# Token sums of the FFN: the eight additions of hi and lo on GpSimd instead of VectorE

## The chip, the cores and the metric

The kernel runs on one core of one Trainium2 chip. The metric is the device time of one execution in microseconds (us), the median over runs. A core has a matrix engine (TensorE, PE in the profile; PEld is its loading of weights), a vector engine (VectorE, DVE), an activation engine (ScalarE, ACT), a general engine (GpSimd, POOL) and an engine that here only issues DMAs (SyncE, SP). Each works through its own queue in order; between the queues semaphores hold an instruction until what it needs is there.

## What is computed

A trunk of two layers over 512 tokens of width 1024: a token mixer (dilated attention in layer 0, a gated recurrence in layer 1) and behind each a gated FFN with a causal convolution of three taps. The change lies in the two FFNs alone:

```python
def conv_ffn(x, w_up, conv_w, conv_b, w_down):
    u = causal_dwconv(x @ w_up, conv_w, conv_b)
    g, v = u[..., :D_FF], u[..., D_FF:]
    return (jax.nn.gelu(g, approximate=True) * v) @ w_down
```

with `D_FF` = 3072, so `x @ w_up` is 512 x 1024 by 1024 x 6144.

## The kernel before

**Numbers in two parts.** Each float32 operand is split into hi, a rounded copy that TensorE multiplies at full speed, and lo, what is left: `split` (lines 148 to 150) copies hi on ACT (L149) and subtracts on DVE (L150). A product is three matmuls, hi by hi, hi by lo and lo by hi (`mm3`, `PASSES`). The normalized tokens lie turned, features on partitions, in the pair `hT`; weights come from DRAM as `raw` and are split into `whi` and `wlo`.

**Products with seven multiplications.** Of the 24 chunks of `w_up`, the first 6 are multiplied plainly (`feat_tiles`, `tiles`; L412). The other 18, the "chains", are cut into two by two blocks and multiplied in seven steps instead of eight (Strassen's scheme in Winograd's form): `chain` (lines 1010 to 1045), run by `seven` (lines 1047 to 1094), matmuls at L1023. The right factors of four of the seven steps are not blocks of the tokens but sums and differences of blocks. They are the same for all chains and are made once in each FFN by `token_sums` (lines 918 to 978). With the four blocks of the tokens, B11 (features 0 to 511, tokens 0 to 255), B12, B21 and B22, each of two tiles of 128x512, it goes through these steps:

- L939, in `both`: each of the eight tiles of the B's is put together as hi + lo from `hT` (`whole` makes the two tiles of a block);
- L957: b11 = B11 - B12, split into the pair T0, right factor of step 5 (`parted(0)`);
- L964 and L945: b12 = B22 - B12 and b22 = -b11 - B22 in turn; b22 is split into T1, factor of step 6 (`parted(1)`), and b12 into T2, factor of step 7 (`parted(2)`);
- L976, run as L945 by the helper `negative`: b21 = -b22 - B21, split into T3, factor of step 4 (`parted(3)`).

The tiles that hold T0 to T3 (`homes`) take the place of the residual stream `x_sb`, which is copied to DRAM first by a DMA from POOL's queue (`x_kept`, L923).

**What sets the order.** The order on every engine is that in which the program issues (`tc.manual_schedule()`). `token_sums` is a side routine: `side` puts it into a list with a delay, and every `tick` (lines 377 to 386), called once for each tile of output, counts the delays down and lets a side routine that is due issue its next part, up to its next `yield n`, which says after how many ticks it goes on. Behind the side routines `tick` calls `pump`, which splits the next weights into free slots and starts loads. In an FFN `token_sums` starts at the fifth tick (line 830). The first eight ticks are two passes over four tiles, one for each half of the tokens (`feat_tiles` with `halves`); six ticks of one full tile each follow (`tiles`, line 831 on), and then `seven` starts. In `seven` the steps of a chain stand at the slots `AT = {1: 0, 5: 1, 2: 2, 6: 4, 3: 5, 7: 8, 4: 13}`.

**The work around it.** A finished tile of `x @ w_up` goes through `begin`: ACT evacuates the bank and applies the third tap (L773, tile `u`), DVE adds the other two taps from the bank (L777, two instructions), then either ACT applies the gelu (L795), or DVE multiplies by the gate (L799). In a chain, L1032 copies the result of step 1 (`part`) out of the bank before step 6 adds onto it; `across` (L210) and `lower` (L214) sum blocks of the raw weights on DVE, and `add_rows` (L186) adds rows to raw weights by an accumulating DMA issued from POOL.

Of the kernel before, what the change touches and what calls it, by code (L numbers as in the profile page):

```python
# [11 lines left out]
F32 = mybir.dt.float32  # L12
# [3 lines left out]
ALU = mybir.AluOpType  # L16
# [67 lines left out]
def kernel(  # L84
# [25 lines left out]
    nc = tc.nc  # L110
# [12 lines left out]
    def nm(s):  # L123
        uid[0] += 1
        return f"{s}{uid[0]}"

    def gen(dt=F32, s="g"):
        return gp.tile([P, 512], dt, tag="g", name=nm(s))
# [19 lines left out]
    def split(hi, lo, raw):  # L148
        nc.scalar.activation(hi, raw, AF.Copy)  # L149
        nc.vector.tensor_tensor(lo, raw, hi.bitcast(F32), op=ALU.subtract)  # L150
# [613 lines left out]
    def ffn(layer, hT, post, pre):  # L764
# [63 lines left out]
        up["direct"] = direct  # L828
        T = []
        side(token_sums(hT, T), 5)  # L830
        for j in range(SEVEN[0] - 1):
            if j:
# [85 lines left out]
    def token_sums(hT, T, first=False):  # L918

        if not first:  # L920
            assert len(sides) == 1, len(sides)
            d = dp.tile([P, 4, D], F32, name=nm("x_kept"))
            nc.gpsimd.dma_start(d, X[0])  # L923
            kept.append(d)
        homes = cp.tile([P, 4, D], F32R, tag="x_sb", name=nm("T"))
        homes = [homes[:, n] for n in range(4)]
        homes += [cp.tile([P, D], F32R, tag="gain", name=nm("T"), bufs=2) for _ in range(1 if first else 2)]
        homes = [[h[:, 0:512], h[:, 512:1024]] for h in homes]
        if first:
            homes += [[gen(F32R, "T") for _ in range(2)]]  # L930
        homes += [[wp.tile([P, 512], F32R, tag=t, name=nm("T")) for _ in range(2)] for t in ("hi", "lo")]
        state["live"] += 2
        homes = [[h.rearrange("p (k t) -> p k t", k=2) for h in hs] for hs in homes]
        yield 1 + first

        def both(k0, n):
            o = gen(s="B").rearrange("p (k t) -> p k t", k=2)
            hi, lo = (h[:, k0 : k0 + 2, n * 256 : n * 256 + 256] for h in hT)
            tt(o, hi.bitcast(F32), lo.bitcast(F32), op=ALU.add)  # L939
            return o  # L940

        tt = nc.vector.tensor_tensor

        def negative(o, a, b):
            nc.vector.scalar_tensor_tensor(o, a, -1.0, b, op0=ALU.mult, op1=ALU.subtract)  # L945

        def whole(k0, n):
            return [both(k0 + 2 * k, n) for k in range(2)]

        def parted(n, b):  # L950
            for k in range(2):
                split(homes[2 * n][k], homes[2 * n + 1][k], b[k])

        b11, b12 = whole(0, 0), whole(0, 1)
        yield 1 + first
        for k in range(2):
            tt(b11[k], b11[k], b12[k], op=ALU.subtract)  # L957
        parted(0, b11)
        yield 1 + first
        b22 = whole(4, 1)  # L960
        if not first:
            yield 1
        for k in range(2):
            tt(b12[k], b22[k], b12[k], op=ALU.subtract)  # L964
            negative(b22[k], b11[k], b22[k])
        yield 1 + first
        parted(1, b22)
        T.extend([homes[2 * n], homes[2 * n + 1]] for n in range(4))
        yield 1 + first
        parted(2, b12)  # L970
        yield 1 + first
        b21 = whole(4, 0)
        if first:
            yield 2
        for k in range(2):
            negative(b21[k], b22[k], b21[k])  # L976
        yield 1 + first
        parted(3, b21)
# [117 lines left out]
    def attention(hT, post, pre):  # L1096
# [359 lines left out]
        for hp in range(4):  # L1456
            q, k = [], []
            if hp % 2 == 0:
                v = []
                values(v) if hp else first_values(v)  # L1460
            if hp == 0:
                side(build)
                side(token_sums(hT, T, True), 2)
            sink = qk_sink(q, k)
            if hp < 3:
                feat_tiles(2, hT, sink)
                for hh in range(2):
                    side(local(2 * hp + hh, hh, q, k, v), 1 + hh)
# [252 lines left out]
```

## Time and profile before

| | |
|---|---|
| median of 3 runs | 1420.02 us (1419.88 to 1420.48) |
| the profiled execution | 1420.89 us |
| its span, first to last instruction | 1419.1 us |
| mean granted TensorE clock | 0.998 |
| additions at L939, DVE | 24 (8 in attention, 8 in each FFN), 684 ns each in the middle |
| token sums' instructions, first FFN | 512.6 to 547 us of the span |
| the same, second FFN | 1054.3 to 1089 us |

A line of the profile's timeline has the start in us from the first instruction, the time that a merged group of instructions spans, the engine, the line of the kernel, the operation, the written tile `<-` the tiles read, their shapes and how many instructions are merged; in brackets stands how long the engine was idle before, and which engine's instruction ended that. A line of the view of waits has the waiting engine and line, what it waited for, and then the total in us, the number of waits and the longest one. A line of the groups has after the bar the busy time in us, the mean in ns, and the idle time ahead.

### The profile page before, as it was taken

The page shows a single profiled execution, that of the slowest core. Times are in us where ns is not written, and L with a number is a line of the kernel's source. Part 1 is how long each engine was busy: PE and PEld are TensorE (multiplying, and loading weights), DVE is VectorE, ACT ScalarE, POOL GpSimd, SP SyncE. Part 2 cuts the span into 40 slices and gives each one's busy share as a digit, 9 for nine tenths or more (in the row PEclk, how much of TensorE's full clock was granted, in tenths as well). Part 3 has the DMA queues.
Part 4 walks back from the last instruction along what each step waited for, and adds up shares of the span by engine and source line. Part 5 has one row for each costly group of instructions (what it writes and reads, how often), then busy time and mean ns, then how long its engine had stood idle before and what let it go on. Part 6 is the DMA issues. An engine that isn't in the chain of part 4 may idle for free.

```text
span 1419.1 us, 23634 instructions
## 1 busy us (share of the span) xinstructions
PE 1406.0 (99%) x8741; PEld 1267.6 (89%) x8741; DVE 1125.1 (79%) x2201; ACT 800.6 (56%) x1646; POOL 225.8 (16%) x344
## 2 busy tenths in 40 slices
PE   9999999999999999999999999999999999999998
PEld 7888999999998898999999888888898999999886
DVE  6676898887866988998888758769789898888843
ACT  7343565353636555666666645589455666666641
POOL 0441332131300102221110001000101212111000
PEclk9999999999999999999999999999999999999999
DMA  7643464655655445666663632431435757665411
GB/s 227 181 145 110 122 178 150 174 162 162 177 184 186 160 149 115 152 153 159 128 151 89 212 129 90 134 119 63 145 127 113 171 118 164 153 130 127 165 58 60
DMA packets 171886, 201.93 MB, mean 142 GB/s; under 512 B 10561, under 2 KB 141081, under 8 KB 171513
## 3 DMA queue, kind: packets, MB, share of 16 engines
q1 hardware_dynamic: 123064, 153.34, 33.8%
q0 software_dynamic: 47856, 46.02, 17.6%
q8 instruction: 69, 1.13, 0.3%
q10 hardware_dynamic: 848, 1.05, 0.2%
q14 instruction: 49, 0.39, 0.1%
HBM read 181.41 MB, written 18.96 MB: 141 GB/s over the span
## 4 chain that ended last, share of the span: by engine, by line
PE 83%; DVE 9%; ACT 5%; issue 1%; DMA 0%; POOL 0%; DVEq 0%; ACTq 0%
PE ps L1023 35%; PE acc L412 25%; PE ps L412 11%; PE v L1219 7%; DVE wlo L150 3%; DVE u L777 2%; PE v L1157 1%; DVE xb L1524 1%; PE O L1431 1%; PE S L1365 1%; ACT whi L149 1%; PE S L1313 1%; DVE T L150 1%; DVE B L939 1%; ACT sig L1545 1%
## 5 line engine op out<-in xcount | busy, mean ns | idle before, releaser
L150 DVE TENSOR_TENSOR wlo<-raw,whi 128x512 fp32r<-128x512 f32 x620 | 410.7, 686 | 112.1 <-ACT whi L149 109.5
L149 ACT ACTIVATE whi<-raw 128x512 fp32r<-128x512 f32 x620 | 371.0, 626 | 189.3 <-PE ps L1023 76.3
L1023 PE MATMUL ps<-T,whi 128*128 128x256 f32 x1664 | 304.3, 283 | 4.2 <-ACT part L1032 3.5
L412 PE MATMUL ps<-hT,whi 128*128 128x512 f32 (+1 forms) x1088 | 288.0, 353 | 0.0
L1023 PEld LDWEIGHTS ps<-T,whi 128*128 128x128 f32 x1664 | 259.3, 190 | 8.9 <-ACT part L1032 3.9
L1023 PE MATMUL ps<-T,wlo 128*128 128x256 f32 x832 | 233.3, 280 | 0.0
L1023 PE MATMUL ps<-hT,whi 128*128 128x256 f32 x1248 | 231.4, 284 | 0.0
L412 PEld LDWEIGHTS ps<-hT,whi 128*128 128x128 f32 x1088 | 190.8, 189 | 26.4
L1023 PEld LDWEIGHTS ps<-hT,whi 128*128 128x128 f32 x1248 | 196.6, 192 | 2.6
L412 PE MATMUL ps<-hT,wlo 128*128 128x512 f32 (+1 forms) x544 | 191.3, 352 | 0.0
L1023 PE MATMUL ps<-hT,wlo 128*128 128x256 f32 x624 | 176.8, 283 | 0.0
L186 POOL DMA_DIRECT2D raw<-in_ffn_w_up_dram x72 | 92.8, 1318 | 424.4 <-DVE wlo L150 291.2
L1023 PEld LDWEIGHTS ps<-T,wlo 128*128 128x128 f32 x832 | 158.4, 190 | 0.0
L412 PE MATMUL acc<-whi,ahi 128*128 128x512 f32 x352 | 137.7, 391 | 0.0
L412 PE MATMUL acc<-whi,alo 128*128 128x512 f32 x352 | 137.2, 390 | 0.2
L412 PE MATMUL acc<-wlo,ahi 128*128 128x512 f32 x352 | 137.0, 389 | 0.0
L1023 PEld LDWEIGHTS ps<-hT,wlo 128*128 128x128 f32 x624 | 119.8, 192 | 0.0
L412 PEld LDWEIGHTS ps<-hT,wlo 128*128 128x128 f32 x544 | 102.9, 189 | 14.0
L1219 PE MATMUL v<-whi,hT 128*128 128x512 f32 x320 | 106.5, 396 | 0.0
L1032 ACT ACTIVATE part<-ps 128x256 f32<-128x256 f32 x156 | 58.7, 376 | 71.7 <-PE ps L1023 68.7
L777 DVE SCALAR_TENSOR_TENSOR u<-ps,cols,u 128x511 f32<-128x511 f32 x120 | 89.4, 746 | 5.0 <-ACT u L773 2.9
L412 PEld LDWEIGHTS acc<-whi,alo 128*128 128x128 f32 x352 | 66.1, 188 | 14.9 <-DVE alo L150 1.1
(206 smaller groups left out, 2125.5 us busy)
## 6 DMA issues: line engine op xcount, KB each, us to landing
raw<-in_ffn_w_up_dram SPq DMA_DIRECT2D x48, 1024.0 KB
raw<-in_attn_w_qkv_dram SPq DMA_DIRECT2D x67, 512.0 KB
raw<-in_ffn_w_up_dram POOLq DMA_DIRECT2D x72, 256.0 KB, 4.9
raw<-in_ffn_w_down_dram SPq DMA_DIRECT2D x14, 1024.0 KB
dw<-in_ffn_w_down_dram SPq DMA_DIRECT2D x40, 256.0 KB
raw<-in_lru_w_in_dram SPq DMA_DIRECT2D x8, 1024.0 KB
turned<-T POOLq DMA_DIRECT2D x26, 256.0 KB, 2.6
ft<-turned POOLq DMA_DIRECT2D x104, 64.0 KB, 4.6
```

What stands on the lines that cost most here:

```text
L149: nc.scalar.activation(hi, raw, AF.Copy)
L150: nc.vector.tensor_tensor(lo, raw, hi.bitcast(F32), op=ALU.subtract)
L186: nc.gpsimd.dma_start(to, src, accum_op=ALU.add)
L412: mm(dst, l[a], r[b], start=start and n == 0, stop=stop and n == 2)
L777: nc.vector.scalar_tensor_tensor(u[:, d:], ps[:, : S - d], wc, u[:, d:], op0=ALU.mult, op1=ALU.add)
L939: tt(o, hi.bitcast(F32), lo.bitcast(F32), op=ALU.add)
L1023: mm(dst, W[wa][0][:, k, :], right[n](ha, k), start=n in (1, 5) and k == q == 0, stop=k == 3 and q == 2, skip_group_check=True,)
L1032: later(1, lambda: nc.scalar.activation(to, dst, AF.Copy))
L1157: mm(banks[t], hT[a][:, k, t * P : (t + 1) * P], W[b][k % 2][:, 0, :], start=u == n == 0, stop=u == 3 and n == 5,)
L1219: mm(bank, hT[a][:, k, t * P : (t + 1) * P], W[b][k % 2][:, 0, :], start=(k, a, b) == (0, 0, 0), stop=(k, a, b) == (KD - 1, 1, 0),)
L1313: mm(Sp[a // 2][:, o + lo : o + 256], q[hh][:, a * P : (a + 1) * P], k[hh][:, k0 : (a + 1) * P], start=True, stop=True)
L1365: mm(ps[:, c], q[hh][:, c], k[hh][:, c], start=True, stop=True)
```

## The change

In the calls from the two FFNs (`first` is False) the eight additions are issued on `nc.gpsimd` instead of `nc.vector`, all eight at the tick at which `token_sums` starts, directly behind the `x_kept` DMA on POOL's queue. The order is B11, B12, B22, B21. The other steps follow from two ticks later on, one step to a tick: b11 - b12 at the tick of before, and from b22 - b12 on each a tick earlier than before. In the call from attention (`first` is True) the engine, the order and the ticks are as they were.

```diff
         homes = [[h.rearrange("p (k t) -> p k t", k=2) for h in hs] for hs in homes]
-        yield 1 + first
+        if first:
+            yield 2
 
         def both(k0, n):
             o = gen(s="B").rearrange("p (k t) -> p k t", k=2)
             hi, lo = (h[:, k0 : k0 + 2, n * 256 : n * 256 + 256] for h in hT)
-            tt(o, hi.bitcast(F32), lo.bitcast(F32), op=ALU.add)
+            (nc.vector if first else nc.gpsimd).tensor_tensor(o, hi.bitcast(F32), lo.bitcast(F32), op=ALU.add)
             return o
...
         b11, b12 = whole(0, 0), whole(0, 1)
-        yield 1 + first
+        if not first:
+            b22, b21 = whole(4, 1), whole(4, 0)
+        yield 2
         for k in range(2):
             tt(b11[k], b11[k], b12[k], op=ALU.subtract)
         parted(0, b11)
         yield 1 + first
-        b22 = whole(4, 1)
-        if not first:
-            yield 1
+        if first:
+            b22 = whole(4, 1)
         for k in range(2):
             tt(b12[k], b22[k], b12[k], op=ALU.subtract)
             negative(b22[k], b11[k], b22[k])
...
         parted(2, b12)
         yield 1 + first
-        b21 = whole(4, 0)
         if first:
+            b21 = whole(4, 0)
             yield 2
         for k in range(2):
             negative(b21[k], b22[k], b21[k])
```

## The prediction

> **What bounds the kernel now.** I read the page first, then TensorE's waits over the whole run.
>
> ```profile
> span 1419.1 us, 23634 instructions
> PE 1406.0 (99%) x8741; PEld 1267.6 (89%) x8741; DVE 1125.1 (79%) x2201; ACT 800.6 (56%) x1646; POOL 225.8 (16%) x344
> ```
>
> ```profile
> PE ps L1023 <- ACT part L1032: 3.5, 2, 1.8
> PE warm L1640 <- DVE one L1685: 1.5, 1, 1.5
> PE ps L1023 <- DVE ps L1041: 0.7, 1, 0.7
> PE v L1157 <- DVE wlo L150: 0.2, 1, 0.2
> ```
>
> TensorE is busy 99% of the span and is named in four rows of waits only. Work taken off VectorE (DVE) is therefore worth something only where it shortens one of them. The first row is two stalls of 1.8 us, one in each FFN, and both stand right behind the token sums that the change touches. TensorE's timeline shows them:
>
> ```profile
> 550.07 0.40 PE L1023 MATMUL ps<-hT,whi 128*128 128x256 f32 x2
> ...
> 552.36 0.50 PE L1023 MATMUL ps<-T,whi 128*128 128x256 f32 x2 [1.77 <-ACT part L1032]
> ...
> 553.77 0.63 PE L1023 MATMUL ps<-T,whi 128*128 128x256 f32 x2
> ...
> 554.41 0.63 PE L1023 MATMUL ps<-hT,whi 128*128 128x256 f32 x2
> ...
> 556.83 0.40 PE L1023 MATMUL ps<-T,whi 128*128 128x256 f32 x2
> ```
>
> ```profile
> 1091.39 0.40 PE L1023 MATMUL ps<-hT,whi 128*128 128x256 f32 x2
> ...
> 1091.75 0.40 PE L1023 MATMUL ps<-hT,whi 128*128 128x256 f32 x2
> ...
> 1094.03 0.50 PE L1023 MATMUL ps<-T,whi 128*128 128x256 f32 x2 [1.77 <-ACT part L1032]
> ...
> 1096.98 0.40 PE L1023 MATMUL ps<-T,whi 128*128 128x256 f32 x2
> ```
>
> A group of three matmuls (two with whi, one with wlo) starts each 0.36 us (1091.39, 1091.75). So the group of 552.36 was due at 550.43 and is 1.93 late; that of 1094.03 was due at 1092.11 and is 1.92 late. In the first FFN the next eight groups take 4.47 us (552.36 to 556.83), in the second 2.95 (1094.03 to 1096.98): behind the first stall a group takes 0.64 us (553.77, 554.41), the clock having dropped, and that costs another 1.52. **All that the change can win is 1.93 + 1.52 + 1.92 = 5.4 us.**
>
> What ends the stall is read on ScalarE (ACT) and DVE:
>
> ```profile
> 546.43 0.64 ACT L795 ACTIVATE u<-u 128x512 f32<-128x512 f32 x1 [1.48 <-DVE u L777]
> 546.97 0.76 ACT L773 ACTIVATE u<-ps,cols 128x512 f32<-128x512 f32 x1
> ...
> 549.38 0.64 ACT L149 ACTIVATE whi<-raw 128x512 fp32r<-128x512 f32 x1 [1.13 <-DVE raw L214]
> 550.88 0.63 ACT L795 ACTIVATE u<-u 128x512 f32<-128x512 f32 x1 [0.87 <-DVE u L777]
> ...
> 551.94 0.36 ACT L1032 ACTIVATE part<-ps 128x256 f32<-128x256 f32 x1
> ```
>
> ```profile
> 540.60 1.28 DVE L939 TENSOR_TENSOR B<-hT,hT 128x512 f32<-128x512 f32 x2
> ...
> 549.26 1.53 DVE L777 SCALAR_TENSOR_TENSOR u<-ps,cols,u 128x511 f32<-128x511 f32 x2
> ```
>
> Step 6 adds onto the bank that step 1's part copy (L1032) has to read first. That copy stands in ACT's order behind the gelu of 550.88, which waits for the taps of 549.26 on DVE; the bank of these taps was evacuated at 547.73 (546.97 + 0.76), 1.53 earlier. DVE is late, and the stall moves one for one with the start of these taps.
>
> **The change, part by part.** Only the calls in the two FFNs change; the one in attention keeps its engine and its order. In each FFN eight additions of 128x512 leave DVE and go to GpSimd (POOL) behind the x_kept copy. The other token steps keep their order, those from b22 - b12 on a tile earlier. Nothing else is issued, and no DMA is added.
>
> ```profile
> 500.69 3.69 DVE L150 TENSOR_TENSOR wlo<-raw,whi 128x512 fp32r<-128x512 f32 x6
> 505.85 1.53 DVE L777 SCALAR_TENSOR_TENSOR u<-ps,cols,u 128x511 f32<-128x511 f32 x2 [1.47 <-ACT u L773]
> 509.94 1.29 DVE L150 TENSOR_TENSOR wlo<-raw,whi 128x512 fp32r<-128x512 f32 x2 [2.56 <-ACT whi L149]
> 511.15 1.53 DVE L777 SCALAR_TENSOR_TENSOR u<-ps,cols,u 128x511 f32<-128x511 f32 x2
> 512.60 2.49 DVE L939 TENSOR_TENSOR B<-hT,hT 128x512 f32<-128x512 f32 x4
> 515.00 1.28 DVE L150 TENSOR_TENSOR wlo<-raw,whi 128x512 fp32r<-128x512 f32 x2
> ...
> 524.35 1.29 DVE L939 TENSOR_TENSOR B<-hT,hT 128x512 f32<-128x512 f32 x2
> 525.55 1.29 DVE L150 TENSOR_TENSOR wlo<-raw,whi 128x512 fp32r<-128x512 f32 x2
> ```
>
> ```profile
> 512.78 0.63 ACT L795 ACTIVATE u<-u 128x512 f32<-128x512 f32 x1 [1.68 <-DVE u L777]
> 513.31 1.14 ACT L149 ACTIVATE whi<-raw 128x512 fp32r<-128x512 f32 x2
> ```
>
> *Removed from DVE.* The pair at 524.35 frees 1.20 us (to 525.55), the pair at 540.60 as much. The four at 512.60 fill 2.4 us, but the split behind them at 515.00 needs ACT's whi, which waits behind the gelu of the taps of 511.15: the two whi of 513.31 take 1.14, the first is done near 513.95, so only 1.05 comes out. Together 1.05 + 1.20 + 1.20 = 3.45 us earlier at the taps of 549.26, and 1.93 is enough to clear the stall. Moving the last splits a tile earlier changes nothing there: they stand ahead of these taps in either order.
>
> *Added on POOL.* Its queue, of before:
>
> ```profile
> 495.18 0.56 POOL L923 DMA_DIRECT2D x_kept<-x_sb  x1 [15.96 <-DVE x_sb L580]
> 517.08 1.32 POOL L186 DMA_DIRECT2D raw<-in_ffn_w_up_dram  x1 [21.34 <-DVE u L777]
> ```
>
> The adds start when the last hT is written, as the six splits of 500.69 begin. POOL has nothing else until the adding transfer of 517.08. No row has a 128x512 addition on POOL; the nearest are its copies in attention, with DVE idle, on 8 partitions (I take it that 128 run side by side as these do):
>
> ```profile
> L1109 POOL COPY row<-rb 8x1 f32<-8x1 f32 x5 | 0.7, 175 | 0.1
> L1109 POOL COPY row<-rb 8x30 f32<-8x30 f32 x2 | 0.4, 200 | 0.0
> L1109 POOL COPY row<-rb 8x8 f32<-8x8 f32 x1 | 0.2, 181 | 0.0
> ```
>
> 29 more elements cost 25 ns, 0.86 each, so 512 cost 0.44 us. An addition reads two operands: at least 0.88 us, and 1.32 if the result passes as a third. I take the middle, 1.1 us; eight with the splits between them (8 x 1.1 + 6 x 0.6 from 500.8) end near 513.2, before the 517.08 transfer and far ahead of b11 - b12.
>
> *What that does to DVE* decides the sum, and one place shows both engines at once:
>
> ```profile
> 47.95 0.66 POOL L1109 COPY row<-rb 8x8 f32<-8x8 f32 x1
> ```
>
> ```profile
> 47.88 2.49 DVE L150 TENSOR_TENSOR wlo<-raw,whi 128x512 fp32r<-128x512 f32 x4
> ```
>
> The copy that takes 0.18 alone took 0.66 here and ended at 48.61, with the first of the four splits (47.88 + 0.68): it waited for a whole DVE instruction, then got in between two. The four splits took 2.49, as four additions do at 512.60, so eight elements on POOL cost DVE nothing visible. What 512 elements on POOL cost a split is not in the trace: between nothing (DVE has the right of way) and the whole addition (each engine holds the other off in turn). I take the whole addition, since the holding off shown is by the instruction. Each of the last five splits then waits for one addition.
>
> By the Trainium skill (SBUF — State Buffer, Who interferes with whom) a DVE instruction with two SBUF inputs and a GpSimd instruction that reads SBUF exclude each other, the later one blocking for the whole of the other. The wait of the copy agrees in one direction; the other, which speaks against this change, no run here shows. The Trainium skill (GPSIMD Engine Reference, Elementwise — side-by-side cycle accounting) has 2.6 cycles per element at 1.2 GHz for such an addition, an estimate of 1.11 us for 512, by which the sum below would be the same.
>
> *Sum.* Five waits of 1.1 make the splits end 5.5 later; the 1.47 idle ahead of the taps of 505.85 absorbs its part, so these start 4.03 late, as does all behind them through ACT's gelu to 511.15. Less 3.45, the taps of 549.26 start **0.58 us later** (in general 5p - 4.92 for a wait p). The stall grows by that in each FFN: +1.2 us. With p at 0.88 and 1.32: -0.52 and +1.68 each, -1.0 and +3.4 together. The profiled execution took 1420.9 us, span 1419.1 and 1.8 around it, 0.9 above the median of 1420.0; it would become 1422.1, and the median **1421.2**. The weights split at 500.69 are used from 513.5 on, so their lateness alone stalls nothing.
>
> **Rivals.**
> (a) *DVE isn't held up.* POOL takes only the gaps; it then runs mostly in DVE's idle 1.47 and 2.56 us and beside the taps, whose one input is in PSUM. The taps of 549.26 go as early as their bank allows (547.73 or sooner, since the gelu of 546.43 ahead of the evacuation waits for DVE too), the part copy comes in time, and both stalls go: 1420.0 - 5.4 = 1414.6. For it: the four splits at 47.88 lost nothing. Against: eight elements may have fitted between two instructions, 512 can't.
> (b) *POOL keeps the port.* The additions stand back to back in its queue; if a waiting split doesn't get in between them, the second split waits for all eight: 8.8 us in place of 5.5, 3.3 more at 549.26. That is +0.58 + 3.3 = 3.9 in each FFN, 7.8 in all, and with 1.5 for a clock drop in the second FFN too, which a longer stall makes likelier, 1429. For it: nothing in the trace shows POOL giving way once it has begun. Against: the copy was let in at the first boundary of DVE. Between my forecast and this, slower by more than 2.8 us starts at p = 1.27, or at 1.12 where the second FFN's clock drops as well.
> (c) *The additions start late*, behind a B buffer's former reader or x_kept. Then b11 - b12 at the head of DVE's order waits; x_kept was issued at 495.18 and the former readers lie in norms that end before hT is complete, so I hold it unlikely; each us late past 518 is a us on the stall.
>
> **How the numbers follow.** A measurement of this kernel tells a change from none at about 0.2%, 2.8 us. Forecast (turns, p from 0.88 to 1.32): 0.47, of which 0.33 within 0.2%, 0.12 slower (upper p, or the second clock drop) and 0.02 faster (lower p, the first clock drop gone: -1.0 - 1.5). (a) 0.33, faster. (b) 0.15, slower. (c) 0.05, split 0.03 slower and 0.02 within. So faster 0.35, within 0.35, slower 0.30. The likeliest case's own range is 1418 to 1425 with a clock drop won or added; the range for 8 in 10 reaches past (a) with 1 us to spare and halfway to (b): 1413.5 to 1426.5.
>
> **What would show it.** On the profile after: the eight additions on POOL near 501 to 513, 1.1 to 1.8 us each with their waits; the six splits that took 3.69 us stretched to about 9 with durations near 1.7 (in (a) they stay 0.68; in (b) one of them lasts near 9); the taps of 505.85 near 510; those of 549.26 near 549.8 and TensorE's stall near 2.3 us. If the wait for L1032 is gone from TensorE's rows, (a) was right and my step on the port wrong; if the splits stretch as said and the time still falls, the step from the splits to the taps of 549.26 was wrong.

## The result and the profile after

The changed kernel takes 1431.22 us (median of 4 runs, 1429.38 to 1431.55) against 1419.95 us before on the same chip: a ratio of 1.0076, 95% interval 1.0059 to 1.0094, or 11.3 us more. It is slower by well over 0.2%, and the time lies above the range that was forecast (1413.5 to 1426.5 us). The profiled execution took 1431.26 us.

```profile
span 1429.5 us, 23631 instructions
PE 1409.3 (99%) x8741; PEld 1270.9 (89%) x8741; DVE 1132.6 (79%) x2185; ACT 800.1 (56%) x1646; POOL 250.1 (17%) x360
```

On this page VectorE has 16 instructions less than before and yet 7.5 us more busy time (1132.6 against 1125.1). An instruction that waits for the other engine counts as busy while it waits, so the profile shows contention as longer instructions, not as idle time.

TensorE's waits in the changed kernel, the rows on the FFNs:

```profile
PE ps L1025 <- ACT part L1034: 6.6, 2, 3.3
PE tr L502 <- DVE xs L485: 3.3, 2, 1.6
```

The stall that stood there before (now L1034, two lines further down in the code) has nearly doubled. The second row is new: TensorE waits in the last norm ahead of each FFN, before the token sums should have touched anything. GpSimd's timeline and then VectorE's, after:

```profile
495.18 0.56 POOL L923 DMA_DIRECT2D x_kept<-x_sb  x1 [15.97 <-DVE x_sb L580]
495.75 2.55 POOL L940 TENSOR_TENSOR B<-hT,hT 128x512 f32<-128x512 f32 x2
502.45 9.80 POOL L940 TENSOR_TENSOR B<-hT,hT 128x512 f32<-128x512 f32 x6 [4.15 <-DVE hT L507]
```

```profile
495.65 3.21 DVE L481 TENSOR_TENSOR xs<-x_sb,gain 128x512 f32<-128x512 f32 x1
...
502.89 9.92 DVE L150 TENSOR_TENSOR wlo<-raw,whi 128x512 fp32r<-128x512 f32 x6
...
552.68 1.53 DVE L777 SCALAR_TENSOR_TENSOR u<-ps,cols,u 128x511 f32<-128x511 f32 x2
```

The two additions of B11 need tokens 0 to 255 alone, which are turned long before the last norm is through. They start at 495.75, and L481 of that norm, which multiplies by the gain, took 3.21 us. Before, the same instruction stood at the same time:

```profile
495.66 0.68 DVE L481 TENSOR_TENSOR xs<-x_sb,gain 128x512 f32<-128x512 f32 x1
```

It ended 0.56 us after the second addition (495.65 + 3.21 = 498.86, 495.75 + 2.55 = 498.30), about its own length: it waited for both. The other six additions start with the last hT, and there the six splits went from 3.69 to 9.92 us. One instruction at a time, GpSimd's and VectorE's timelines of the changed kernel read:

```profile
503.71 1.74 POOL L940 TENSOR_TENSOR B<-hT,hT 128x512 f32<-128x512 f32 x1
505.41 1.75 POOL L940 TENSOR_TENSOR B<-hT,hT 128x512 f32<-128x512 f32 x1
```

```profile
502.89 1.41 DVE L150 TENSOR_TENSOR wlo<-raw,whi 128x512 fp32r<-128x512 f32 x1
...
504.22 1.78 DVE L150 TENSOR_TENSOR wlo<-raw,whi 128x512 fp32r<-128x512 f32 x1
505.93 1.78 DVE L150 TENSOR_TENSOR wlo<-raw,whi 128x512 fp32r<-128x512 f32 x1
```

The engines take turns in a period of 1.70 us: a split waits 1.10 us for an addition (1.78 in place of 0.68), an addition 0.47 us for a split (1.74 in place of the 1.27 that each of the first pair took). Only the first split, which found its addition already under way, waited less: 0.73 us (1.41 in place of 0.68).

TensorE's timeline of the changed kernel shows what that costs (and, behind it, the one row of before that is not yet shown):

```profile
500.03 1.09 PE L502 MATMUL tr<-ident,xs 128*128 128x128 f32 x8 [1.65 <-DVE xs L485]
...
555.78 0.79 PE L1025 MATMUL ps<-T,whi 128*128 128x256 f32 x2 [3.32 <-ACT part L1034]
...
561.07 0.60 PE L1025 MATMUL ps<-T,whi 128*128 128x256 f32 x2
...
1101.84 0.80 PE L1025 MATMUL ps<-T,whi 128*128 128x256 f32 x2 [3.33 <-ACT part L1034]
...
1107.12 0.63 PE L1025 MATMUL ps<-T,whi 128*128 128x256 f32 x2
```

```profile
498.21 1.04 PE L502 MATMUL tr<-ident,xs 128*128 128x128 f32 x8
```

Three terms make the loss, both FFNs alike. The norm's transposes come 1.82 us later (500.03 against 498.21): 3.6 us. The stall for L1034 grows from 1.77 to 3.32 us: 3.1 us. And the clock drops behind both stalls, not behind one (the granted clock is 0.50 from 557 to 561 us and from 1103 to 1107): eight groups of three matmuls take 5.29 us (555.78 to 561.07) and 5.28 us (1101.84 to 1107.12), against 4.47 and 2.95 before: 0.8 + 2.3 us. Together 9.8 of the 10.4 us between the spans; some of the rest is the ninth group behind each stall, still slow (0.55 us to the next start in the first FFN, against 0.36).

### The profile page after: what moved, and what is told of

The parts are those of the page before. It is cut to its first block, busy times and chain, and to the rows that moved or that the text cites. A ratio compares the mean times of both kernels' runs of the same rounds, so it can differ in the third digit from the quotient of the medians.

```text
span 1429.5 us, 23631 instructions
## 1 busy us (share of the span) xinstructions
PE 1409.3 (99%) x8741; PEld 1270.9 (89%) x8741; DVE 1132.6 (79%) x2185; ACT 800.1 (56%) x1646; POOL 250.1 (17%) x360
## 4 chain that ended last, share of the span: by engine, by line
PE 71%; issue 14%; DVE 10%; DMA 2%; ACT 1%; POOL 0%; DVEq 0%; POOLq 0%; ACTq 0%
PE ps L1025 35%; PE acc L412 18%; PE ps L412 8%; PE v L1221 6%; DVE wlo L150 3%; DVE u L777 2%; PE v L1159 1%; DMA ft<-turned 1%; PE S L1367 1%; PE S L1315 1%; PE O L1433 1%; DVE T L150 1%; ACT whi L149 0%; PE O L412 0%; DVE hT L507 0%
## 5 line engine op out<-in xcount | busy, mean ns | idle before, releaser
L150 DVE TENSOR_TENSOR wlo<-raw,whi 128x512 fp32r<-128x512 f32 x620 | 423.0, 705 | 117.2 <-ACT whi L149 114.7
L1034 ACT ACTIVATE part<-ps 128x256 f32<-128x256 f32 x156 | 58.7, 376 | 75.8 <-PE ps L1025 73.8
L455 POOL DMA_DIRECT2D turned<-T x34 | 18.6, 550 | 355.4 <-DVE T L449 353.7
```

Of the source, the lines that this page charges most:

```text
L455: nc.gpsimd.dma_start(d, T)
L1034: later(1, lambda: nc.scalar.activation(to, dst, AF.Copy))
```

## The experiments

Two theories were set against each other. E: the two engines hold each other off where both read operands from SBUF, early in the norm (L481) and then at the six splits. O: it is the new order, the earlier ticks or the buffers, and not the engine. Differences below are to the runs of the kernel before on the same chip (its median there in brackets); those with one run of their own are good to about 1.5 us, since 13 runs of the kernel before on one chip spread from 1419.30 to 1422.42.

### No addition inside the norm

```diff
-        b11, b12 = whole(0, 0), whole(0, 1)
-        if not first:
-            b22, b21 = whole(4, 1), whole(4, 0)
+        if first:
+            b11, b12 = whole(0, 0), whole(0, 1)
+        else:
+            b12, b22, b11, b21 = whole(0, 1), whole(4, 1), whole(0, 0), whole(4, 0)
```

> The changed kernel with the eight GpSimd additions in the order B12, B22, B11, B21, so that the first waits for the last tokens' hT and none can start inside the last norm. Theory E (engines hold each other off): the change costs two things in each FFN, 1.8 us by B11's additions at 495.75 holding up the norm's multiplication (L481 took 3.21 us instead of 0.68), the rest by the six splits behind hT. Then L481 is back at 0.68 us, TensorE's wait for L485 goes, the splits still stretch to about 9 to 10 us, the stall for L1034 stays near 3 us, and the time is 1424 to 1428 us. Rival O (it is the order and the earlier ticks, not the engine): 1431 us, as the changed kernel.

1425.09 us (1420.97): ratio 1.0029, interval 1.0018 to 1.0040, 4.1 us more. VectorE's timeline and TensorE's, of this kernel:

```profile
496.47 0.68 DVE L481 TENSOR_TENSOR xs<-x_sb,gain 128x512 f32<-128x512 f32 x1
...
501.50 9.93 DVE L150 TENSOR_TENSOR wlo<-raw,whi 128x512 fp32r<-128x512 f32 x6
...
551.32 1.53 DVE L777 SCALAR_TENSOR_TENSOR u<-ps,cols,u 128x511 f32<-128x511 f32 x2
```

```profile
554.41 0.50 PE L1026 MATMUL ps<-T,whi 128*128 128x256 f32 x2 [3.01 <-ACT part L1035]
...
558.86 0.41 PE L1026 MATMUL ps<-T,whi 128*128 128x256 f32 x2
...
1097.30 0.50 PE L1026 MATMUL ps<-T,whi 128*128 128x256 f32 x2 [3.01 <-ACT part L1035]
...
1101.76 0.40 PE L1026 MATMUL ps<-T,whi 128*128 128x256 f32 x2
```

L481 is back at 0.68 us, TensorE's wait in the norm is gone, and the splits stretch as before. As theory E expected, the order of the four blocks alone, which decides whether an addition can start inside the norm, is worth several us: 11.3 - 4.1 = 7.2 by the medians, each against its own chip's runs of before. The spans of the two profiled executions are 5.6 us apart (1429.5 and 1423.9), and the rows account for 5.9: 3.6 for the norm's transposes, 0.6 for the stalls (3.32 against 3.01 us), 1.7 for the groups behind them (5.29 against 4.45 us). What is left is the splits: the stall is 3.01 us, 1.24 more than before, in both FFNs, and the second FFN has a clock drop too, worth 1.5 us (eight groups take 4.45 us from 554.41 on and 4.46 from 1097.30 on; before, the second FFN had 2.95): 2 x 1.24 + 1.5 = 4.0 us, against 4.1 measured.

### The same order on VectorE

```diff
-            (nc.vector if first else nc.gpsimd).tensor_tensor(o, hi.bitcast(F32), lo.bitcast(F32), op=ALU.add)
+            tt(o, hi.bitcast(F32), lo.bitcast(F32), op=ALU.add)
```

> The changed kernel with all eight additions back on VectorE, at the places of the change (all at the first tick, the other steps behind them as in the change). Theory E: they stand behind the taps of 505.85 where VectorE idles 2.56 us, so four of eight cost nothing there; taps of 549.26 about 1.2 us earlier than before, stall about 0.6 us, no clock drop in the first FFN: 1415 to 1418 us. Rival O: no faster than 1420 and up to 1431 us. A third, that the place of the additions does not matter as long as VectorE does them: 1419.5 to 1420.5 us.

1417.28 us (1420.97): ratio 0.9976, interval 0.9966 to 0.9986. This undoes the engine and keeps everything else of the change, and it is 3.7 us faster than before: O falls. VectorE's timeline and TensorE's:

```profile
507.89 4.90 DVE L940 TENSOR_TENSOR B<-hT,hT 128x512 f32<-128x512 f32 x8
```

```profile
551.69 0.51 PE L1025 MATMUL ps<-T,whi 128*128 128x256 f32 x2 [0.51 <-ACT part L1034]
```

The eight additions stand in the 2.56 us in which VectorE waited for ACT; half of them cost nothing there. The stall falls to 0.51 us in both FFNs and no clock drop follows it: 2 x 1.26 + 1.5 = 4.0 us, against 3.7 measured.

### GpSimd's additions behind the splits

```diff
+        if not first:
+            lo = list(units.values())[-1][1][-1]
+            nc.gpsimd.tensor_copy(small(1), lo[:, 0, 0:1].bitcast(F32))
         b11, b12 = whole(0, 0), whole(0, 1)
```

> The changed kernel with one more instruction on GpSimd ahead of its additions, a copy of one column of the latest split's lo, so that they start when the six splits are done, in the stretch where VectorE idles and does taps. Theory E: the six splits take 3.7 us again, additions from 504.4 to about 515, the splits of 509.94 wait for one or two additions (2 us), taps of 549.26 1 to 1.5 us earlier than before, stall at most 0.9 us: 1415 to 1419 us. Rival O: 1431 us.

1416.74 us (1420.97): ratio 0.9970, interval 0.9960 to 0.9981, 4.2 us faster. GpSimd's timeline, VectorE's, and TensorE's:

```profile
505.60 0.19 POOL L957 COPY s<-wlo 128x1 f32<-128x1 f32 x1 [8.70 <-DVE wlo L150]
505.74 10.95 POOL L940 TENSOR_TENSOR B<-hT,hT 128x512 f32<-128x512 f32 x8
```

```profile
501.84 3.69 DVE L150 TENSOR_TENSOR wlo<-raw,whi 128x512 fp32r<-128x512 f32 x6
507.00 1.53 DVE L777 SCALAR_TENSOR_TENSOR u<-ps,cols,u 128x511 f32<-128x511 f32 x2 [1.47 <-ACT u L773]
511.09 3.20 DVE L150 TENSOR_TENSOR wlo<-raw,whi 128x512 fp32r<-128x512 f32 x2 [2.56 <-ACT whi L149]
```

```profile
551.99 0.50 PE L1028 MATMUL ps<-T,whi 128*128 128x256 f32 x2 [0.25 <-ACT part L1037]
```

The splits are undisturbed. So are the taps (1.53 us) that run beside the additions: one of their two large operands is in PSUM. Only the two splits of 511.09 pay, 3.20 us in place of 1.29. TensorE's stall is 0.25 us. With the same eight additions on the same engine the time moves from 11.3 us more to 4.2 us less by their start alone. (The 4.2 us here and the 3.7 us of the same order on VectorE are not told apart by their intervals.)

A variant in two parts, B11 and B12 behind the six splits, and B22 and B21 a tick later behind the next two:

> As e3, but in two parts: the additions of B11 and B12 on GpSimd behind the six splits, those of B22 and B21 a tick later behind the next two splits, each held by a copy of one column. Theory E: the two splits that took 3.20 us in e3 take 1.3 again, the taps of 549.26 come early enough to clear the last 0.3 us of the stall in each FFN: 1415.5 to 1416.7 us. If the last additions run into the splits behind them instead: 1416.5 to 1418 us.

1417.70 us (1420.98), ratio 0.9979, interval 0.9970 to 0.9989: no better. The second expectation held: the splits of 511 took 1.29 us again, and the next two, at 514.96, took 3.53.

### Unused work on GpSimd

Three kernels are the kernel before, VectorE keeping its eight additions, with work on GpSimd at the place of the change whose results nobody reads: additions, memsets, copies.

```diff
+        if not first:
+            for k0, n in ((0, 0), (2, 0), (0, 1), (2, 1), (4, 1), (6, 1), (4, 0), (6, 0)):
+                hi, lo = (h[:, k0 : k0 + 2, n * 256 : n * 256 + 256].bitcast(F32) for h in hT)
+                nc.gpsimd.tensor_tensor(gen(s="dummy").rearrange("p (k t) -> p k t", k=2), hi, lo, op=ALU.add)
         yield 1 + first
```

> The kernel before, with eight additions of the same shape and operands added on GpSimd at the same place, whose results nobody reads; VectorE keeps its own eight. Theory E: the price of holding off alone, with no work taken from VectorE: L481 3.2 us, the six splits near 10 us, the taps of 549.26 about 3.4 us later still than in the changed kernel, stall for L1032 near 6.5 us with a clock drop: 1437 to 1442 us. Rival O: additions that nobody waits for cost nothing, 1420 us.

1437.38 us (1420.97): ratio 1.0115, interval 1.0095 to 1.0135, within the expected 1437 to 1442 us. TensorE's waits:

```profile
PE ps L1027 <- ACT part L1036: 13.6, 2, 6.8
```

So the additions cost 16.4 us by being there, and the change, which takes VectorE's eight away and issues the later steps earlier, gives back some 5 us of it. The memsets write only:

```diff
+        if not first:
+            nc.gpsimd.tensor_copy(small(1), hT[1][:, 7, 511:512].bitcast(F32))
+            for n in range(16):
+                nc.gpsimd.memset(gen(s="dummy"), 0.0)
```

> The kernel before, with sixteen memsets of 128x512 on GpSimd, whose results nobody reads, at the place of the additions and held behind the last tokens' hT by a copy of one column. They write and read nothing. Theory R (it is the reading of SBUF that the two engines can't do together): the six splits stay at 3.7 us, 1420 us. Rival W (any GpSimd instruction holds VectorE off): with a memset near 0.5 us each the splits take 6 us or more, and the time is above 1422 us.

1419.62 us in one run (1420.98). GpSimd, then VectorE:

```profile
501.56 7.52 POOL L937 MEMSET dummy<- 128x512 f32 x16
```

```profile
500.89 3.69 DVE L150 TENSOR_TENSOR wlo<-raw,whi 128x512 fp32r<-128x512 f32 x6
```

Writing beside the splits costs them nothing. (The time itself says less than the rows: both stalls are 1.78 us here, 1.77 before, and in this execution neither was followed by a clock drop.) The copies read one operand, `hi`, and replace the addition by `nc.gpsimd.tensor_copy`:

> The kernel before, with eight copies of 128x512 (one operand read, hi alone) on GpSimd, whose results nobody reads, in place of the eight unused additions. Theory R: they hold the splits off too, but for less: a copy near 0.5 to 0.6 us, L481 near 1.8 us, the six splits near 6 us, so 1424 to 1431 us, between the kernel before and the 1437 us of the unused additions. Rival (only an addition, with two operands, holds VectorE off): 1420 us.

1424.53 us in one run (1420.98). GpSimd, then VectorE:

```profile
496.56 1.17 POOL L938 COPY dummy<-hT 128x512 f32<-128x512 f32 x2
500.81 4.78 POOL L938 COPY dummy<-hT 128x512 f32<-128x512 f32 x6 [3.08 <-ACT hT L506]
```

```profile
496.48 1.80 DVE L481 TENSOR_TENSOR xs<-x_sb,gain 128x512 f32<-128x512 f32 x1
...
502.32 5.01 DVE L150 TENSOR_TENSOR wlo<-raw,whi 128x512 fp32r<-128x512 f32 x6
```

They hold VectorE off too, for less: L481 by 1.12 us, the splits by 1.3, where 2.3 had been expected; the six copies, which need `hi` alone, began 1.5 us ahead of the splits (500.81). In these runs it is GpSimd's reading of SBUF that excludes a VectorE instruction with two operands in SBUF: the splits took 9.92 us beside additions, 5.01 beside copies and 3.69 beside memsets, and the taps, with one large operand in PSUM, kept their 1.53. The Trainium skill (SBUF — State Buffer, Who interferes with whom) states just this, that an instruction that only writes does not contend included; the runs agree on both counts.

### One addition, or all that stand there?

L481 waited for two additions, each split for one. Four additions that have their tokens early tell whether that was chance:

```diff
+            b11, b21, b12, b22 = whole(0, 0), whole(4, 0), whole(0, 1), whole(4, 1)
```

> The changed kernel with the order B11, B21, B12, B22, so that four additions, not two, have their tokens before the last norm is through. In the changed kernel the norm's multiplication at L481 waited for two additions in a row. Theory S (additions that stand back to back don't let VectorE in once they have begun): it waits for all four, L481 near 5.7 us, TensorE's wait for L485 near 4.2 us in each FFN, and the six splits find only four additions left: 1433 to 1437 us. Rival A (they always take turns, and the second wait had another cause): L481 stays at 3.2 us or below, TensorE's wait for L485 at 1.65 us.

1427.87 us in one run (1420.98), so the expected time was missed. VectorE, then TensorE, then TensorE's clock (the column behind POOL's count in the view by stretches):

```profile
495.95 5.64 DVE L481 TENSOR_TENSOR xs<-x_sb,gain 128x512 f32<-128x512 f32 x1
```

```profile
502.75 1.97 PE L502 MATMUL tr<-ident,xs 128*128 128x128 f32 x8 [4.09 <-DVE xs L485]
```

```profile
504.00:506.00 2.00, 2.00 (x11) 2.00 (x10) 1.81 (x4) 1.74 (x4) 0.70 (x1) 0.50 0.00 0
```

The mechanism of S held: L481 waited for all four. The time did not, because waits replace one another: TensorE, 4.1 us later in the norm, with its clock drop there (0.50 in the row above), meets a VectorE that has since caught up, and no row of its waits names the part copy any more.

Two more kernels ask what decides between one and all (in brackets stands here a single run of the kernel before), first with an unused multiplication of two operands in SBUF right behind L481:

> The changed kernel with one more VectorE multiplication of two 128x512 operands in SBUF directly behind L481 of the last norm, its result unread. In the changed kernel L481 waited for both additions of B11, while each of the six splits waited for one. Theory Q (a VectorE instruction gets in between two additions where another of its kind stands behind it): L481 now ends after the first addition, near 1.9 us, and the extra one after the second. Rival P (an instruction that comes before the first addition of a run waits for the whole run, whatever stands behind it): L481 stays at 3.2 us and the extra one takes 0.68 us. In time both are near the changed kernel's 1431 us, up to 2 us more.

```profile
496.50 3.20 DVE L481 TENSOR_TENSOR xs<-x_sb,gain 128x512 f32<-128x512 f32 x1
499.62 0.68 DVE L483 TENSOR_TENSOR extra<-x_sb,gain 128x512 f32<-128x512 f32 x1
```

P held (1429.80 us in one run, 1422.04). The other had a memset of 0.5 us ahead of the additions:

> The changed kernel with one memset of 128x512 (0.52 us) on GpSimd between the x_kept copy and the additions, its result unread, so that the first addition starts when L481 is nearly done. If only L481's coming first made it wait for two: L481 is back at 0.68 us, and the norm's next instructions, of 128x1 (L425 to L428), are held up by one addition at most, so that TensorE's wait for L485 falls below 1.65 us. If the norm is held up for the whole run wherever it meets it: one of L425 to L485 takes 1.9 to 2.7 us and the wait stays near 1.65 us. 1426 to 1431 us.

1428.34 us in one run (1422.04). GpSimd, then VectorE:

```profile
496.25 2.55 POOL L940 TENSOR_TENSOR B<-hT,hT 128x512 f32<-128x512 f32 x2
```

```profile
495.69 0.68 DVE L481 TENSOR_TENSOR xs<-x_sb,gain 128x512 f32<-128x512 f32 x1
496.29 1.31 DVE L425 SCALAR_TENSOR_TENSOR s<-s,s 128x1 f32<-128x1 f32 x1
497.52 0.15 DVE L426 RECIPROCAL s<-s 128x1 f32<-128x1 f32 x1
497.70 1.12 DVE L427 SCALAR_TENSOR_TENSOR s<-s,s 128x1 f32<-128x1 f32 x1
```

L481 is free, and instead two instructions of 128x1, 0.15 and 0.22 us long before, wait for one addition each, while the reciprocal between them, with one operand, kept its 0.15; TensorE's wait in the norm falls from 1.65 to 1.2 us. In all these runs a VectorE instruction with two operands in SBUF whose recorded start lies up to 0.1 us ahead of the first addition or copy waits for the whole run of two or four, and one that comes while an addition runs waits for that one. The prediction has from the Trainium skill (SBUF — State Buffer, Who interferes with whom) that the later of the two blocks for the whole of the other; the splits bear that out, and L481, whose start is recorded first and which waited for all, does not. Whether it was really first is not shown, since 0.1 us between the records of two engines is little, and why it does not get in between two additions stays open.

## Why the prediction was wrong

- *What bounds the kernel, and what can be won:* right. The stall moved one for one with the taps of 549.26: in the change the taps are 3.42 us later (552.68), and TensorE is 1.82 us later with a stall that is 1.55 us longer, 3.37 together. The kernels that bring these taps forward win 3.7, 4.2 and 3.3 of the 5.4 us.
- *"The adds start when the last hT is written":* **this is the step that failed.** The program waits by slices, B11 reads tokens 0 to 255, and its additions had nothing to wait for behind x_kept at 495.18; the row was quoted and not asked what it lets start. So the queue was followed forward to 517.08 but what ran on VectorE from 495.18 on was never listed. It is worth 7.2 of the 11.3 us by the medians of the first experiment (5.6 between the profiled executions): L481, the norm, TensorE's transposes, and with them a longer stall and a longer drop of the clock.
- *"Each of the last five splits then waits for one addition", p = 1.1:* the price was right, 1.10 us by the period of 1.70, but in part by luck: it was the middle between two bounds for the addition's length, and an addition takes 1.27 us alone, near the upper bound (and above the estimate of 1.11 us from the Trainium skill, GPSIMD Engine Reference, Elementwise — side-by-side cycle accounting); a split waits 0.17 us less than that. The count was one short, since the first split waited too, 0.73 us. With B11 held back, the stall grew by 1.24 us against 0.58 forecast, and the difference of 0.66 is nearly that 0.73. The rest of the path, the 1.47 us of idle time that absorb and the 3.45 us that come out, was right: 5 x 1.10 + 0.73 - 1.47 - 3.45 = 1.31 us, against 1.24.
- *The clock drop in the second FFN* was named as a chance, in rival (b) and beside the forecast, and left out of the sum; it came (1.5 us with B11 held back, 2.3 in the change). These three, 7.2 + 2 x 0.66 + 1.5 = 10.0 us, are nearly the whole of the 10.1 us between the 1.2 that was forecast and the 11.3 measured.
- *Rival (b), "POOL keeps the port":* half right. Additions back to back did pass over a waiting instruction, but in the norm and not at the splits, where the engines took turns as forecast.
- *Rival (a):* refuted by the six splits, 9.92 us in place of 3.69; its best sign, the four undisturbed splits at 47.88, was of eight elements and said nothing of 512. *Rival (c)* had the wrong sign: the additions started early.
- *The range:* its upper end, 1426.5, lies two thirds of the way from 1421.2 to the 1429 of rival (b), not halfway as the prediction says; the measured time is above either.

## What to carry to other kernels

Moving work to an idle engine moves it in time as well: ask for each moved instruction when its inputs are ready at the earliest, and what runs then. GpSimd instructions that read SBUF belong beside VectorE instructions with an operand in PSUM, or in VectorE's idle time, and may have to be held back for it (a copy of one column that reads the right tile is enough); the same eight additions cost 11.3 us or win 4.2 by their start alone. Before moving work at all, look whether its own engine idles a little earlier: the new order on VectorE gave 3.7 us without GpSimd, as much within the noise.

## What was not expected of the hardware

Behind a stall of the same length, 1.77 us, TensorE's clock fell to half in the first FFN of the kernel before and not in the second, in the same execution. The view by stretches has the granted clock behind POOL's count:

```profile
554.00:556.00 2.00, 2.00 (x11) 2.00 (x11) 1.91 (x4) 1.48 (x4) 0.16 (x1) 0.50 0.24 59
1095.50:1097.50 2.00, 2.00 (x19) 2.00 (x19) 1.90 (x4) 1.49 (x4) 0.00 (x0) 1.00 0.64 92
```

Over the profiles of all these kernels, from 130 us of the span on, the clock fell behind each of TensorE's eleven stalls of 3.0 us and more, behind four of the nine from 1.77 to 2.26, and behind none of those from 0.8 to 1.67. What decides in between is not shown.

A VectorE instruction on a single column waits as long for a GpSimd addition as one on 512 columns (1.31 us in place of 0.15, against 1.78 in place of 0.68).
